# Last gates, split of y, conditioning columns and GpSimd work in a decoder trunk

## The chip, the cores and the metric

The kernel runs on one core of a Trainium2 chip. The metric is the time of one execution on the device, in microseconds (us). Six engines matter here: PE (TensorE, matmuls), DVE (VectorE), ACT (ScalarE), POOL (GpSimd) and the queues of DMAs that SP (SyncE) and POOL issue. Each engine works its own instructions strictly in the order in which they stand; it waits at an instruction until what this needs is there.

## The reference, cut to what matters

A trunk of two layers over x of 1024 positions by 1024 channels. Each sub-layer is a norm with scale and shift from a conditioning vector, a mixer or an MLP, and a gated residual add:

```python
for i in range(2):
    mod = einsum("bd,de->be", silu(c), w_mod[i]) + b_mod[i]
    sh_m, sc_m, gt_m, sh_f, sc_f, gt_f = split(mod, 6)
    h = rms_norm(x, norm_mix_g[i]) * (1 + sc_m) + sh_m
    y = recurrent_mixer(h, ...) if i == 0 else pool_mixer(h, ...)
    x = x + gt_m * y
    h = rms_norm(x, norm_ffn_g[i]) * (1 + sc_f) + sh_f
    x = x + gt_f * (relu(h @ w1[i]) ** 2 @ w2[i])
out = rms_norm(x, final_norm_g)

def recurrent_mixer(h, ...):
    gate = gelu(h @ w_y + b_y)
    xr = causal_conv4(h @ w_in + b_in)
    r, g = sigmoid(heads(xr, w_a)), sigmoid(heads(xr, w_x))   # 4 heads of 256
    log_a = 8 * r * log_sigmoid(lam)
    xr = scan(exp(log_a), sqrt(-expm1(2 * log_a)) * g * xr)   # along the sequence
    return (xr * gate) @ w_out + b_out
```

All of it is float32.

## The kernel before

Activations lie transposed, 128 channels on the partitions and positions along the free axis, in two halves of 512 positions (h = 0 and 1; tiles `xa` and `xb`). A float32 product is made of three: an operand is split into a high part, rounded to a type that PE multiplies fast, and a low part, the rest. One 128x512 block over 1024 channels, `proj`, is thus 24 matmuls (lines 188 to 190). A high part is an ACT copy, a low part a DVE or POOL subtraction, or, for weights in the variant "dma" (`neg_part`), an ACT negation onto which a DMA of POOL's queue adds the weights once more.

Weights come as units of 512 KB by SP's queue into three raw buffers (`rawp`), and split into eight half-unit tiles (`wpool`). The conditioning vectors `mod[i, j]` are made of columns: `drip` loads 512 KB of `w_mod` into one of the same three raw buffers (tile `mb`) and multiplies and sums them on DVE (line 207). `rate[0]` says how many columns `split_unit` drips with each unit.

The mixer of layer 0 ends with four heads. Per head and half, `gates` splits its input (tile `xchl`, from a pool of 19 slots that `yh` and `yl` share), makes 24 matmuls, four sigmoids, and on ACT, POOL and DVE exp, tanh, square root and scan; `gelu_block` makes 48 matmuls, two gelus and the products. `split_y(h)` splits the result into `yh` and `yl`. Then the projection `w_out` runs in two groups of four output blocks, each over both halves; each block is evacuated by ACT, added to x by DVE and squared into a sum (`SumSq`) whose plan gives each addition to V (DVE) or G (POOL). `ffn_norm` adds up the sum on PE (line 272), broadcasts the reciprocal root (line 286), and `norm_split` makes `hh` and `hl`, for three of eight blocks (`lean`) with POOL. The FFN's first product `f1` of both halves follows, then `f2`.

A scheduler puts the instructions of each engine in order from the order in the code, its own estimates of when things are ready, and the free buffers; the lines alone don't show it.

Of the kernel before, what the change touches and what calls it, by code (L numbers as in the profile page):

```python
# [10 lines left out]
F32 = mybir.dt.float32  # L11
F32R = mybir.dt.float32r
AF = mybir.ActivationFunctionType
# [29 lines left out]
def trunk_kernel(ctx, tc, xT, vecs, wmod, w_k, w_in, w_y, w_g, w_out, w_p, w1, w2, outT):  # L43
    nc = tc.nc
    V, S, G, PE = nc.vector, nc.scalar, nc.gpsimd, nc.tensor
# [44 lines left out]
    x = [Blocks("xa"), Blocks("xb")]  # L90
# [66 lines left out]
    rate = [0]  # L157
# [10 lines left out]
    def split_unit(src, name, eng=None, drips=None):  # L168
        raw = load(src, name)
        drip(rate[0] if drips is None else drips)  # L170
        if eng == "dma":
            return [neg_part(raw[:, c:c + H], src[:, c:c + H], f"{name}_{c}") for c in (0, H)]
        return [split_part(raw[:, c:c + H], f"{name}_{c}", eng) for c in (0, H)]
# [26 lines left out]
    mod = {}  # L200
# [28 lines left out]
    def drip(n):  # L229
        for _ in range(n):  # L230
            next(steps, None)
# [56 lines left out]
            trace[S], trace[V] = root, last  # L288
        return bc

    def norm_split(x, bc, a, b, hh, hl, lean=()):
        for k in range(NB):
            t = tmp("nt")
            V.scalar_tensor_tensor(t, x[:, k, :], a[:, k:k + 1], bc, op0=ALU.mult, op1=ALU.mult)  # L294
            if k in lean:
                S.activation(t, t, AF.Identity, bias=b[:, k:k + 1])
                S.copy(hh[:, k, :], t)
                G.tensor_sub(hl[:, k, :], t, hh[:, k, :].bitcast(F32))
                continue
            last = (S.activation(hh[:, k, :], t, AF.Identity, bias=b[:, k:k + 1]),  # L300
                    V.scalar_tensor_tensor(hl[:, k, :], t, b[:, k:k + 1], hh[:, k, :].bitcast(F32),  # L301
                                           op0=ALU.add, op1=ALU.subtract))
        return last


    hh, hl = [None, None], [None, None]
# [11 lines left out]
    a, b = const.tile([P, NB], F32, name="amix0"), mod_tile(0, 0)  # L318
# [70 lines left out]
    for k in range(NB):  # L389
# [17 lines left out]
        for low, r in ((0, hh), (0, hl), (1, hh)):  # L407
            for u in range(6):
                w, c = (w1_, u * P) if u < 4 else (w2_, odd * 256 + (u - 4) * P)
# [101 lines left out]
    def gates(hd, unit, h):  # L511

        xchl = slot("xchl", (2, 2, H), F32R)
        xch, xcl = xchl[:, 0, :, :], xchl[:, 1, :, :]
        src = xc[h][:, 2 * hd:2 * hd + 2, :]
        S.copy(xch, src)
        V.tensor_sub(xcl, src, xch.bitcast(F32))
        rs, gs = [], []
        for mi in range(2):
            b = 2 * hd + mi  # L520
            for g in range(2):
                ps = acc_mm()
                for k in range(2):
                    mm3(ps, unit, ((g * 2 + k) * 2 + mi) * P, xch[:, k, :], xcl[:, k, :], k == 0, k == 1)
                t = tmp("gate")
                S.activation(t, ps, AF.Sigmoid, bias=vcol("ba" if g == 0 else "bx", b))
                (rs if g == 0 else gs).append(t)
        aa = []
        for mi in range(2):
            b = 2 * hd + mi  # L530

            av = tmp("a")
            S.activation(av, rs[mi], AF.Exp, scale=coef[:, b:b + 1])
            S.activation(rs[mi], rs[mi], AF.Tanh, scale=ncoef[:, b:b + 1])
            aa.append(av)
        for mi in range(2):
            e = tmp("asq")
            G.tensor_mul(e, aa[mi], aa[mi])  # L538
            V.scalar_tensor_tensor(rs[mi], e, 1.0, rs[mi], op0=ALU.add, op1=ALU.mult)
        for mi in range(2):  # L540
            b = 2 * hd + mi
            S.activation(rs[mi], rs[mi], AF.Sqrt)
            hs = xc[h][:, b, :]
            G.tensor_mul(gs[mi], gs[mi], hs)
            V.tensor_mul(gs[mi], gs[mi], rs[mi])
            V.tensor_tensor_scan(hs, aa[mi], gs[mi], 0.0 if h == 0 else carry[:, b:b + 1],
                                 op0=ALU.mult, op1=ALU.add)
            if h == 0:
                V.tensor_copy(carry[:, b:b + 1], hs[:, H - 1:H])
# [9 lines left out]
    def split_y(h):  # L559
        yh[h], yl[h] = Blocks(f"yh{h}", F32R), Blocks(f"yl{h}", F32R)  # L560
        for k in range(NB):
            S.copy(yh[h][:, k, :], xc[h][:, k, :])
            V.tensor_sub(yl[h][:, k, :], xc[h][:, k, :], yh[h][:, k, :].bitcast(F32))

    for hd in range(4):
        rate[0] = min(hd, 2)
        ug = split_unit(w_g[hd], f"g{hd}")
        uy = [split_unit(w_y[m], f"y{m}") for m in (2 * hd, 2 * hd + 1)]
        for h in range(2):
            gates(hd, ug, h)  # L570
            for mi in range(2):
                gelu_block(2 * hd + mi, uy[mi], h)
            if hd == 3:
                if h == 1:
                    wo = [split_unit(w_out[m], f"o{m}", G, 0) for m in range(4)]
                split_y(h)

    af = [None, None]

    def ffn_norm(i, h, ss):  # L580
        if af[i] is None:
            drip_until(i, 3)
            af[i] = norm_scale(vcol(f"gffn{i}"), mod[i, 4], f"affn{i}")
        bc = rstd_bcast(ss)
        new_h(h)
        norm_split(x[h], bc, af[i], mod[i, 3], hh[h], hl[h], (1, 3, 5))


    drip_until(0, 2)
    gtb = const.tile([P, NB], F32, name="gtb")  # L590
    V.tensor_mul(gtb, mod[0, 2], vcol("bout"))
    room = slot("ssq")
    ss = [SumSq("f00", plan="GVGVGVGV", room=room[:, 0:2, :]), SumSq("f01", plan="GVGVGVGV", room=room[:, 2:4, :])]
    rate[0] = 4
    for m0 in (0, 4):
        if m0:
            wo = [split_unit(w_out[m], f"o{m}") for m in range(m0, m0 + 4)]
        for h in range(2):
            for m in range(m0, m0 + 4):
                ps = proj(wo[m - m0], yh[h], yl[h])  # L600
                t = tmp("wo")
                S.activation(t, ps, AF.Identity, bias=gtb[:, m:m + 1], scale=mod[0, 2][:, m:m + 1])
                V.tensor_add(x[h][:, m, :], x[h][:, m, :], t)
                ss[h].add(x[h][:, m, :])
                if h == 1 and m == 4:
                    ffn_norm(0, 0, ss[0])

# [81 lines left out]
    def f1_jobs(i, c, eng=None):  # L689
        return [partial(lambda j: split_unit(w1[i, c * 4 + j], f"w1_{i}_{c}_{j}", eng, DRIPS[j]), j) for j in range(4)]  # L690
# [166 lines left out]
    def jobs(i, first, last):  # L857

        for c in range(first, last):
            yield from f1_jobs(i, c, G if (i, c) == (0, 0) else None)  # L860
            yield from f2_jobs(i, c)
        yield from f1_jobs(i, last)

# [93 lines left out]

    sa, sb = SumSq("n0a", plan="GVGVGVGV"), SumSq("n0b", plan="VVVVVVVV")  # L960
    qa, qb = SumSq("f1a", plan="VVVVVVVV"), SumSq("f1b", plan="VVVVVVVV")
    f1(0, 6, AB, fast=True, ahead=ahead)
    drip_until(1, 5)
# [67 lines left out]
    sa = last_chunk(0, 0, H, "GVGVGVGV")  # L1031
    sb = last_chunk(1, 0, n1, "VVVVVVVV", once(lambda: final_norm(rstd_bcast(sa), 0, 0, H)))
# [73 lines left out]
```

## Time and profile before

| | us |
|---|---|
| median of 3 runs | 1766.14 (1762.34 to 1766.17) |
| profiled execution | 1766.89 |
| its span on the core | 1765.1 |
| PE busy | 1704.2 (97%) |
| DVE busy | 1367.9 (77%) |
| ACT busy | 959.7 (54%) |
| POOL busy | 544.3 (31%) |

A busy share is a mean over stages with different limits. PE's idle 61 us lie in a few places, and a matmul counts as busy at either clock, so the granted clock is to be read beside it. The heads of the mixer take about 130 to 275 us of the span, the projection 275 to 371, `f1` of the first FFN chunk 371 to 426.

### The profile page before, as it was taken

The numbers are of one execution on the slowest core, as the hardware profiler recorded it, in microseconds if no ns is written. First come the engines' busy times: TensorE is split into PE (matmuls) and PEld (weight loads), VectorE is DVE, ScalarE is ACT, GpSimd is POOL, SyncE is SP. The second block draws the span as 40 slices with busy tenths as digits, with TensorE's granted clock in tenths as the row PEclk, the third lists the DMA queues.
The fourth block names the chain that finished last, engine by engine and source line by source line (L and its number), as shares of the span: only waits on it lengthen the run. The fifth ranks groups of instructions, "written<-read, shape, count | busy, mean of one in ns | idle before, by whom it ended". The sixth has DMA issues, their size and how long they took to land.

```text
span 1765.1 us, 20959 instructions
## 1 busy us (share of the span) xinstructions
PE 1704.2 (97%) x7510; PEld 1397.7 (79%) x7510; DVE 1367.9 (77%) x2092; ACT 959.7 (54%) x1648; POOL 544.3 (31%) x442
## 2 busy tenths in 40 slices
PE   5899989989999999999999999999999999999997
PEld 3687768778788888888888888888878787878787
DVE  8898866678888888888874698649786968686836
ACT  4578884346354545444456688745444454545432
POOL 4323332151313223241407433312231404140403
PEclk8999999989999999999999999999999999999998
DMA  9223413521424142423217889861111111111202
GB/s 354 90 72 107 144 60 108 190 84 48 140 71 135 60 143 72 132 73 118 84 48 166 196 182 194 171 167 47 61 37 60 54 42 60 48 61 36 78 7 96
DMA packets 59577, 180.80 MB, mean 102 GB/s; under 512 B 6352, under 2 KB 8784, under 8 KB 59472
## 3 DMA queue, kind: packets, MB, share of 16 engines
q1 hardware_dynamic: 47376, 157.43, 27.7%
q0 software_dynamic: 12096, 22.03, 7.5%
q8 instruction: 59, 0.97, 0.2%
q14 instruction: 46, 0.38, 0.1%
HBM read 175.24 MB, written 4.19 MB: 102 GB/s over the span
## 4 chain that ended last, share of the span: by engine, by line
PE 71%; DVE 15%; ACT 5%; DMA 4%; issue 3%; POOL 1%; SPq 0%; DVEq 0%; ACTq 0%; POOLq 0%
PE mm L188 23%; PE mm L189 23%; PE mm L190 23%; DMA mb<-in_wmod 3%; DVE mb L207 2%; DVE mw L333 1%; DVE xca L449 1%; DVE xa L780 1%; PE sm L272 1%; DVE xb L780 1%; POOL xa L789 1%; DVE xcb L449 1%; DVE hl L301 1%; DVE nt L294 1%; POOL asq L538 1%
## 5 line engine op out<-in xcount | busy, mean ns | idle before, releaser
L188 PE MATMUL mm<-hh,w_w 128*128 128x512 f32 x1024 | 400.3, 391 | 1.0 <-DVE xa L780 1.0
L189 PE MATMUL mm<-hl,w_w 128*128 128x512 f32 x1024 | 399.4, 390 | 0.0
L190 PE MATMUL mm<-hh,w_w 128*128 128x512 f32 x1024 | 399.3, 390 | 0.0
L789 POOL TENSOR_TENSOR xb<-xb,c 128x512 f32<-128x512 f32 x104 | 149.8, 1440 | 603.9 <-ACT c L784 558.9
L188 PEld LDWEIGHTS mm<-hh,w_w 128*128 128x128 f32 x1024 | 192.8, 188 | 42.5 <-DVE xa L780 2.7
L190 PEld LDWEIGHTS mm<-hh,w_w 128*128 128x128 f32 x1024 | 192.8, 188 | 40.4
L189 PEld LDWEIGHTS mm<-hl,w_w 128*128 128x128 f32 x1024 | 192.8, 188 | 39.8
L789 POOL TENSOR_TENSOR xa<-xa,c 128x512 f32<-128x512 f32 x104 | 160.0, 1538 | 145.0 <-ACT c L784 145.0
L784 ACT ACTIVATE c<-c,mod 128x512 f32<-128x512 f32 x104 | 75.3, 724 | 204.5 <-DVE c L810 119.0
L207 DVE SCALAR_TENSOR_TENSOR mb<-mb,cond 128x1024 f32<-128x1024 f32 x80 | 115.3, 1442 | 53.7 <-DMA mb<-in_wmod 53.5
L630 ACT ACTIVATE relu<-mm 128x512 f32<-128x512 f32 x128 | 76.3, 596 | 140.8 <-PE mm L190 140.7
L780 DVE SCALAR_TENSOR_TENSOR xa<-mm,mod,xa 128x512 f32<-128x512 f32 x156 | 113.0, 742 | 25.8 <-POOL xa L789 21.0
L181 DVE TENSOR_TENSOR w_w<-raw_w,w_w 128x512 fp32r<-128x512 f32 x112 | 108.5, 977 | 12.0 <-ACT w_w L180 11.7
L165 POOL DMA_DIRECT2D w_w<-in_w x72 | 63.9, 906 | 106.6 <-ACT w_w L164 65.9
L180 ACT CAST w_w<-raw_w 128x512 fp32r<-128x512 f32 x120 | 69.8, 612 | 27.9 <-PE mm L190 20.6
L620 DVE TENSOR_TENSOR u<-usq,u 128x512 fp32r<-128x512 f32 x102 | 70.3, 689 | 17.1 <-ACT u L619 16.7
L188 PE MATMUL mm<-u,w_a_a 128*128 128x512 f32 x200 | 79.1, 396 | 2.2 <-DVE xa L780 1.0
L188 PE MATMUL mm<-u,w_w 128*128 128x512 f32 (+1 forms) x224 | 81.0, 362 | 0.0
L189 PE MATMUL mm<-u,w_w 128*128 128x512 f32 (+1 forms) x224 | 80.6, 360 | 0.1
L190 PE MATMUL mm<-u,w_w 128*128 128x512 f32 (+1 forms) x224 | 80.4, 359 | 0.0
L189 PE MATMUL mm<-u,w_a_a 128*128 128x512 f32 x200 | 78.0, 390 | 0.0
L190 PE MATMUL mm<-u,w_a_a 128*128 128x512 f32 x200 | 77.9, 389 | 0.0
(336 smaller groups left out, 4113.9 us busy)
## 6 DMA issues: line engine op xcount, KB each, us to landing
raw_w<-in_w SPq DMA_DIRECT2D x148, 512.0 KB, 3.6
mb<-in_wmod SPq DMA_DIRECT2D x80, 512.0 KB, 3.7
w_w<-in_w POOLq DMA_DIRECT2D x72, 256.0 KB, 5.5
mw<-in_wmod SPq DMA_DIRECT2D x16, 512.0 KB, 9.2
raw_in<-in_w_in SPq DMA_DIRECT2D x8, 512.0 KB, 3.6
raw_y<-in_w_y SPq DMA_DIRECT2D x8, 512.0 KB, 3.6
raw_o<-in_w_out SPq DMA_DIRECT2D x8, 512.0 KB, 3.7
outT<-o SPq DMA_DIRECT2D x12, 256.0 KB, 2.3
```

Of the source, the lines that this page charges most:

```text
L165: nc.gpsimd.dma_start(w[:, 1, 0:n], src, accum_op=ALU.add)
L180: S.copy(w[:, 0, 0:n], raw)
L181: (eng or V).tensor_sub(w[:, 1, 0:n], raw, w[:, 0, 0:n].bitcast(F32))
L188: PE.matmul(out=ps, lhsT=wh, rhs=rh, start=first, stop=False)
L189: PE.matmul(out=ps, lhsT=wh, rhs=rl, start=False, stop=False)
L190: PE.matmul(out=ps, lhsT=w[:, 1, c:c + P], rhs=rh, start=False, stop=last)
L207: V.scalar_tensor_tensor(raw, raw, 1.0, cond, op0=ALU.mult, op1=ALU.mult, accum_out=m[:, e:e + 1])
L620: eng.tensor_sub(u[n][:, 1, jj, :], src, u[n][:, 0, jj, :].bitcast(F32))
L630: S.activation(r, ps, AF.Relu)
L780: V.scalar_tensor_tensor(xb, ps, g[:, r + 4 * row:r + 4 * row + 1], xb, op0=ALU.mult, op1=ALU.add)
L784: S.activation(t, src, AF.Identity, scale=g[:, r + 4 * row:r + 4 * row + 1])
L789: G.tensor_add(xb, xb, t)
```

## The change

`norm_split` loses `lean`: all eight blocks go the same way, ACT for `hh` and DVE for `hl`. The plans of three sums give all additions to DVE. The weights of the projection's second group and of the FFN's first chunk are split by "dma" instead of by DVE and by POOL. The columns' rate is 0, 1, 2, 3 in the heads (before 0, 1, 2, 2), one after each block of the projection's first group, and 0 with its second group's units (before 4 each). `split_y(0)` stands after the last gates, and the first four units of `w_out` and `split_y(1)` after the heads.

```diff
-    def norm_split(x, bc, a, b, hh, hl, lean=()):
+    def norm_split(x, bc, a, b, hh, hl):
         for k in range(NB):
             t = tmp("nt")
             V.scalar_tensor_tensor(t, x[:, k, :], a[:, k:k + 1], bc, op0=ALU.mult, op1=ALU.mult)
-            if k in lean:
-                S.activation(t, t, AF.Identity, bias=b[:, k:k + 1])
-                S.copy(hh[:, k, :], t)
-                G.tensor_sub(hl[:, k, :], t, hh[:, k, :].bitcast(F32))
-                continue
...
     for hd in range(4):
-        rate[0] = min(hd, 2)
+        rate[0] = hd
         ug = split_unit(w_g[hd], f"g{hd}")
         uy = [split_unit(w_y[m], f"y{m}") for m in (2 * hd, 2 * hd + 1)]
         for h in range(2):
             gates(hd, ug, h)
+            if (hd, h) == (3, 1):
+                split_y(0)
             for mi in range(2):
                 gelu_block(2 * hd + mi, uy[mi], h)
-            if hd == 3:
-                if h == 1:
-                    wo = [split_unit(w_out[m], f"o{m}", G, 0) for m in range(4)]
-                split_y(h)
+    wo = [split_unit(w_out[m], f"o{m}", G, 0) for m in range(4)]
+    split_y(1)
...
-        norm_split(x[h], bc, af[i], mod[i, 3], hh[h], hl[h], (1, 3, 5))
+        norm_split(x[h], bc, af[i], mod[i, 3], hh[h], hl[h])
...
-    ss = [SumSq("f00", plan="GVGVGVGV", room=room[:, 0:2, :]), SumSq("f01", plan="GVGVGVGV", room=room[:, 2:4, :])]
-    rate[0] = 4
+    ss = [SumSq("f00", plan="VVVVVVVV", room=room[:, 0:1, :]), SumSq("f01", plan="VVVVVVVV", room=room[:, 1:2, :])]
+    rate[0] = 0
     for m0 in (0, 4):
         if m0:
-            wo = [split_unit(w_out[m], f"o{m}") for m in range(m0, m0 + 4)]
+            wo = [split_unit(w_out[m], f"o{m}", "dma") for m in range(m0, m0 + 4)]
         for h in range(2):
             for m in range(m0, m0 + 4):
...
                 ss[h].add(x[h][:, m, :])
+                if m0 == 0:
+                    drip(1)
                 if h == 1 and m == 4:
                     ffn_norm(0, 0, ss[0])
...
-            yield from f1_jobs(i, c, G if (i, c) == (0, 0) else None)
+            yield from f1_jobs(i, c, "dma" if (i, c) == (0, 0) else None)
...
-    sa, sb = SumSq("n0a", plan="GVGVGVGV"), SumSq("n0b", plan="VVVVVVVV")
+    sa, sb = SumSq("n0a", plan="VVVVVVVV"), SumSq("n0b", plan="VVVVVVVV")
```

How the scheduler moves the instructions is shown at three places. The line numbers of the changed kernel are five lower from `norm_split` to the projection and three lower behind it.

**The heads, DVE.** Around the scan of head 3, first half, before; `xchl<-xcb` is the input of its second half, `yl` a low part of y:

```order
L539 SCALAR_TENSOR_TENSOR gate<-asq,gate 128x512 x2
L545 TENSOR_TENSOR gate<-gate 128x512 x2
L546 SCALAR_TENSOR_TENSOR xca_469<-a,gate 128x512 x2
L549 COPY carry<-xca_469 128x1 x2
L555 TENSOR_TENSOR xca_469<-xca_469,gelu 128x512
L517 TENSOR_TENSOR xchl<-xcb_471,xchl 128x1024
```

The same instruction now, before the scan of head 2, first half, with the columns (`mb`, line 207) that follow up to the gates of head 2, second half:

```order
L512 TENSOR_TENSOR xchl<-xcb_471,xchl 128x1024
L540 TENSOR_TENSOR gate<-gate 128x512 x2
L541 SCALAR_TENSOR_TENSOR xca_469<-a,gate 128x512 x2
L544 COPY carry<-xca_469 128x1
L207 SCALAR_TENSOR_TENSOR mb_4_6_1826,mod_4_1559<-mb_4_6_1826,cond 128x1024
L544 COPY carry<-xca_469 128x1
L550 TENSOR_TENSOR xca_469<-xca_469,gelu 128x512 x2
L207 SCALAR_TENSOR_TENSOR mb_4_7_1837,mod_4_1559<-mb_4_7_1837,cond 128x1024
L181 TENSOR_TENSOR w_y_0_1829<-raw_y_1818,w_y_0_1829 128x512
L210 TENSOR_TENSOR mod_4_1559<-mod_4_1559,vec 128x8
L240 SCALAR_TENSOR_TENSOR affn_2626<-mod_4_1559,vec 128x8
L207 SCALAR_TENSOR_TENSOR mb_3_0_1842,mod_3_1841<-mb_3_0_1842,cond 128x1024
```

The split of the last gates' input moved some 30 instructions forward, and columns `mb_4_7` and `mb_3_0`, which before stood behind `split_y(1)`, now stand ahead of the gates of head 2, second half, on DVE.

**The projection's second group, first half, DVE.** Before, from its first block on (`xa`, the residual add; `ssq`, the sum of squares):

```order
L207 SCALAR_TENSOR_TENSOR mb_5_5_2462,mod_5_2438<-mb_5_5_2462,cond 128x1024
L603 TENSOR_TENSOR xa_82<-xa_82,wo 128x512
L207 SCALAR_TENSOR_TENSOR mb_5_6_2465,mod_5_2438<-mb_5_6_2465,cond 128x1024
L207 SCALAR_TENSOR_TENSOR mb_5_7_2794,mod_5_2438<-mb_5_7_2794,cond 128x1024
L603 TENSOR_TENSOR xa_82<-xa_82,wo 128x512
L210 TENSOR_TENSOR mod_5_2438<-mod_5_2438,vec 128x8
L263 TENSOR_TENSOR ssq<-ssq,sq 128x512
L207 SCALAR_TENSOR_TENSOR mb_1_0_2807,mod_1_2806<-mb_1_0_2807,cond 128x1024
L603 TENSOR_TENSOR xa_82<-xa_82,wo 128x512 x2
L263 TENSOR_TENSOR ssq<-ssq,sq 128x512
```

Now:

```order
L207 SCALAR_TENSOR_TENSOR mb_5_3_2797,mod_5_2393<-mb_5_3_2797,cond 128x1024
L598 TENSOR_TENSOR xa_82<-xa_82,wo 128x512
L263 TENSOR_TENSOR ssq<-ssq,sq 128x512
L598 TENSOR_TENSOR xa_82<-xa_82,wo 128x512
L263 TENSOR_TENSOR ssq<-ssq,sq 128x512
```

The last pair stands twice more behind these. The columns between the adds are gone there, and every addition of squares stands on DVE.

**The second norm's sum, DVE.** Before, the last adds of the second half (`xb`), up to the reciprocal; `raw_w` are FFN weights:

```order
L603 TENSOR_TENSOR xb_84<-xb_84,wo 128x512
L263 TENSOR_TENSOR ssq<-ssq,sq 128x512
L603 TENSOR_TENSOR xb_84<-xb_84,wo 128x512
L207 SCALAR_TENSOR_TENSOR mb_1_2_2829,mod_1_2806<-mb_1_2_2829,cond 128x1024
L729 TENSOR_TENSOR raw_w_0_0_0_2838<-raw_w_0_0_0_2838 128x256
L603 TENSOR_TENSOR xb_84<-xb_84,wo 128x512
L731 TENSOR_TENSOR raw_w_0_0_0_2838<-raw_w_0_0_0_2838 128x256
L263 TENSOR_TENSOR ssq<-ssq,sq 128x512
L207 SCALAR_TENSOR_TENSOR mb_1_3_2840,mod_1_2806<-mb_1_3_2840,cond 128x1024
L729 TENSOR_TENSOR raw_w_0_0_1_3194<-raw_w_0_0_1_3194 128x256
L276 RECIPROCAL rstd<-rstd 128x4
```

Now:

```order
L207 SCALAR_TENSOR_TENSOR mb_5_5_2823,mod_5_2393<-mb_5_5_2823,cond 128x1024
L263 TENSOR_TENSOR ssq<-ssq,sq 128x512
L598 TENSOR_TENSOR xb_84<-xb_84,wo 128x512
L726 TENSOR_TENSOR raw_w_0_0_0_2834<-raw_w_0_0_0_2834 128x256
L728 TENSOR_TENSOR raw_w_0_0_0_2834<-raw_w_0_0_0_2834 128x256
L263 TENSOR_TENSOR ssq<-ssq,sq 128x512
L207 SCALAR_TENSOR_TENSOR mb_5_6_2836,mod_5_2393<-mb_5_6_2836,cond 128x1024
L598 TENSOR_TENSOR xb_84<-xb_84,wo 128x512
L207 SCALAR_TENSOR_TENSOR mb_5_7_3183,mod_5_2393<-mb_5_7_3183,cond 128x1024
L263 TENSOR_TENSOR ssq<-ssq,sq 128x512
L210 TENSOR_TENSOR mod_5_2393<-mod_5_2393,vec 128x8
```

Before, one column stood here ahead of the last addition; now three do, and there is one addition more.

## Rows read from the trace of the kernel before

**Rows 1.** Waits of PE, 120 to 400 us: total us, times, longest us.

```profile
engine line waited for: us in total, times, longest us
PE mm L188 <- ACT xchl L516: 5.7, 1, 5.7
PE sm L272 <- POOL ssq L263: 4.9, 2, 2.7
PE mm L188 <- ACT gelu L554: 4.0, 4, 1.5
PE sm L272 <- DVE ssq L263: 3.4, 2, 1.9
```

**Rows 2.** Stretches: length, PE busy (matmuls), PE's granted clock, DMA share, GB/s.

```profile
255.30:260.60 5.30, 4.89 (x11) 0.50 0.00 0
...
349.80:356.50 6.70, 6.70 (x23) 0.50 0.00 0
...
382.00:390.60 8.60, 8.58 (x27) 0.50 0.21 69
...
1130.00:1320.00 190.00, 189.96 (x837) 1.00 0.33 85
```

**Rows 3.** Timeline of PE: start us, us, line, out<-in, count; where stages begin.

```profile
249.22 0.39 PE L190 MATMUL mm<-hh,w_y 128*128 128x512 f32 x1
...
274.77 0.39 PE L188 MATMUL mm<-yh,w_o 128*128 128x512 f32 x1
...
371.49 0.39 PE L188 MATMUL mm<-hh,w_w 128*128 128x512 f32 x1
...
426.28 0.39 PE L188 MATMUL mm<-u,w_a_a 128*128 128x512 f32 x1
```

**Rows 4.** Timeline of DVE and ACT in heads 2 and 3, with idle time before.

```profile
226.68 1.22 DVE L207 SCALAR_TENSOR_TENSOR mb<-mb,cond 128x1024 f32<-128x1024 f32 x1 [2.29 <-DMA mb<-in_wmod]
...
235.00 0.69 DVE L539 SCALAR_TENSOR_TENSOR gate<-asq,gate 128x512 f32<-128x512 f32 x1 [0.93 <-POOL asq L538]
...
254.25 1.03 ACT L516 CAST xchl<-xcb 128x1024 fp32r<-128x1024 f32 x1
...
259.94 1.28 ACT L526 ACT_TABLE_LOAD   x1 [0.47 <-PE mm L190]
```

**Rows 5.** Timeline of DVE and POOL at the end of the projection's first half.

```profile
338.60 1.23 DVE L207 SCALAR_TENSOR_TENSOR mb<-mb,cond 128x1024 f32<-128x1024 f32 x1 [1.62 <-DMA mb<-in_wmod]
...
339.75 0.69 DVE L603 TENSOR_TENSOR xa<-xa,wo 128x512 f32<-128x512 f32 x1
...
343.89 1.23 DVE L207 SCALAR_TENSOR_TENSOR mb<-mb,cond 128x1024 f32<-128x1024 f32 x1 [2.06 <-DMA mb<-in_wmod]
...
347.09 1.25 DVE L603 TENSOR_TENSOR xa<-xa,wo 128x512 f32<-128x512 f32 x1 [1.36 <-ACT wo L602]
...
346.53 1.26 POOL L263 TENSOR_TENSOR ssq<-ssq,sq 128x512 f32<-128x512 f32 x1 [8.40 <-ACT sq L262]
```

**Rows 6.** Timeline of DVE between the first norm and the second's sum.

```profile
369.12 3.47 DVE L301 SCALAR_TENSOR_TENSOR hl<-nt,mod,hh 128x512 fp32r<-128x512 f32 x2
...
376.26 2.31 DVE L207 SCALAR_TENSOR_TENSOR mb<-mb,cond 128x1024 f32<-128x1024 f32 x1
```

**Rows 7.** Prices: DMA issues and operations by line, ns min/median/max, landing us.

```profile
mb<-in_wmod SPq DMA_DIRECT2D x80, 512.0 KB, 3.7
...
L165 POOL DMA_DIRECT2D w_w<-in_w x72: 852/872/1667, 938.7 to 1165.9; - x72
...
DMA to landing us min/median/max: 3.8/5.6/8.3
...
1124.03 0.95 PE L272 MATMUL sm<-ones,ssqf1bV 128*128 128x1 f32 x8
...
L301 DVE SCALAR_TENSOR_TENSOR hl<-nt,mod,hh x28: 736/747/1989, 85.4 to 1138.9; 128x512 fp32r<-128x512 f32 x28
```

**Rows 8.** Stretches: length, busy of PE, PEld, DVE, ACT, POOL; clock, DMA, GB/s.

```profile
190.00:250.00 60.00, 58.09 (x254) 47.12 (x252) 45.13 (x62) 54.00 (x76) 25.20 (x18) 1.00 0.38 123
402.00:426.00 24.00, 24.00 (x107) 19.88 (x106) 18.82 (x33) 14.94 (x27) 0.00 (x0) 1.00 0.15 44
```

## The prediction

> **What bounds the kernel now.** PE is busy in 1704 of 1765 us, so only the places where it stands still or runs slowly are worth anything. I read first who PE waited for between 120 and 400 us [rows 1]: once 5.7 us for ACT's copy `xchl` of the last gates, 4.0 us in four pieces for gelu evacuations, and 8.3 us (4.9 and 3.4) at the two sums of squares `ssq` of the next norm. Then the granted clock after each long wait [rows 2]: 0.50, the lower of the two levels (1.2 of 2.4 GHz), from 255.3 to 260.6, from 349.8 to 356.5 and from 382.0 to 390.6. Each long wait is thus paid twice. From 1130 to 1320 PE does 837 matmuls in 189.96 us, 0.227 us each, with no wait: the pace that I charge for undisturbed work. Then when PE starts each stage [rows 3]: its last gelu matmul of head 3, first half, at 249.22, the projection `w_o` at 274.77, the FFN's first product at 371.49, its second at 426.28.
>
> **The ideal.** (A) From 249.45 to the projection stand 24 gate and 48 gelu matmuls, 72 x 0.227 = 16.3 us, so 265.8 instead of 274.77: 9.0 us lost. (B) The projection is 16 blocks of 24, 384 x 0.227 = 87.1 us; with one part of the sum of squares the small matmuls L272 are 8 for 0.95 us [rows 7], the broadcast adds about 0.5: 88.5 against 96.7, 8.2 us lost. (C) The first FFN product is 8 blocks, 43.5 us, plus 1.4 for the second norm's small matmuls: 44.9 against 54.8, 9.9 us lost. More than 27.1 us is not there in these places.
>
> **The change, part by part.**
>
> *Last gates.* ACT casts `xchl` of (3, 1) only at 254.25, after its chain of (3, 0) [rows 4]; the pool of slots is the reason that I read from the code, since the first half's `yh`, `yl` take four slots before it. In the new order `split_y(0)` comes after these gates, and the cast and its subtraction move ahead of the scan of (2, 0), some 35 us earlier. The wait for `xchl` goes. Next late is the ACT chain: between 190 and 250 it is busy 54.0 of 60 us [rows 8], and PE can run ahead of it by six PSUM buffers. Following that chain, the first gelu of (3, 0) frees its buffer about 0.5 us after PE asks for it: 0.5 off.
>
> *Columns in the heads.* Rate 3 instead of 2 puts three more columns into DVE's queue there, 3 x 1.23 us, and their 512 KB loads into SP's ahead of `raw_y` 7. DVE already stands 2.29 us for a column at 226.68 [rows 4]. `mb_4_7` and `mb_3_0` now come through one free buffer, one after the other: `mb_4_6` is done about 224.4, 3.7 us to land [rows 7] and 1.2 to work gives 229.4 and then about 234.4, in front of the first gate operation L539, whose second of the pair moves from 235.00 to about 236.4. The subtractions of `yl` that stood there (3.3 us) have left, or it would be worse. So 1.4 us go to ACT's square root behind it and to PE; from 0, if a buffer comes free sooner, to 5, one more round trip. With the 0.5 above, 2 us off: A gives 7.0.
>
> *Projection.* Before, 16 columns stand between the residual adds of all blocks, 5.3 us apart at 338.60 and 343.89 [rows 5], so the add of the last block of the first half comes at 347.09, though PE finished it near 340, and at 1.25 us instead of 0.69, beside POOL's addition that starts at 346.53. Now the second half has no column behind `mb_5_3`. The first half has seven, and behind `split_y(1)` three raw buffers turn them over; I get the last at about 298, some 15 us after PE ended the block whose add waits behind it, and six PSUM buffers hold 33 us of blocks. When PE asks for the sum at T + 70.7 (T the projection's start), the last sum is ready at about T + 68. B gives its 8.2. Eight DVE subtractions become 8 ACT negations (beside 5.4 us blocks in which ACT has 1.4 us of other work) and 8 transfers from POOL's queue. The first low half: its unit is loaded only behind `mb_5_1`, negated at about 302.5, plus 0.87 us of issue and 5.6 to land [rows 7] = 309; PE wants it at 311.4. Covered by 2 us.
>
> *Norm.* POOL's subtractions and additions go. DVE gets 3 more operations of 0.75 us per norm and 4 more additions per sum, each the size of the add of 0.69 [rows 5]; against that, two L301 took 3.47 us beside POOL's work where their median is 0.747 [rows 6, 7]. The Trainium skill, page "SBUF — State Buffer", section "SBUF: two separate sides", says that the port pair DVE shares with GpSimd is an exclusive lock; that agrees with the 3.47. The same section's box warns that a DVE operation can also keep GpSimd from writing descriptors for its own DMAs, which speaks against the 16 transfers put there; it is a rival below.
>
> *Second norm's sum.* PE reaches it half a block later in the new order. Its chain on DVE has `mb_5_5`, `mb_5_6`, `mb_5_7` in front of the last adds, as `mb_1_2` stood before at 376.26 for 2.31 us [rows 6]. I follow it to T + 97.5 where PE asks at T + 96.9: 1 us off, 0 to 5. C gives 8.9.
>
> *Behind it.* The second norm's output ends some 4 to 5 us later against PE's second half than before, where DVE is busy 18.8 of 24 us [rows 8]. The idle 5.2 us hide it or don't: 0 to 5 off, I take 2.5, the middle.
>
> *Elsewhere.* The pool mixer's first sum loses 8 of 16 small matmuls: 0.95 us won. Three DVE operations more in each norm of the second layer cost nothing while PE doesn't wait there; from 1130 on it has none [rows 2]. The columns end three units later, before their first use. If that cover failed, 3 x 0.75 us each.
>
> **Sum.** The profiled execution took 1766.89 us, 1.8 more than its span; the median of the runs is 1766.14, 0.04% lower, so I don't correct. 7.0 + 8.2 + 8.9 - 2.5 + 0.9 = 22.5: 1766.9 - 22.5 = **1744.4 us**. With the costs at zero it is 27.1 + 0.9 = 28 us, 1738.9. With all at their ends (5.5, 5 and 5, so 3.5 + 8.2 + 4.9 - 5 + 0.9 = 12.5) it is 1754.4.
>
> **Rivals.**
>
> *ACT holds the heads* (chance 0.11). The earlier copy brings nothing, because ACT's chain, 54.0 of 60 us busy, and not `xchl`, sets when PE may go on. For: PE already waits 4.0 us for gelu [rows 1]. Against: ACT's table load at 259.94 waited for PE [rows 4], so ACT could have gone on sooner. A falls out: 1766.9 - 15.5 = 1751.4.
>
> *The second norm's chain stays late* (0.11). The columns 5_5 to 5_7 wait for buffers held by FFN weights, one round trip of 5 us each past the first; PE waits over 4 us at the sum, the clock falls as it did after 382.0, and C is gone: 1766.9 - 13.6 = 1753.3.
>
> *Low halves late* (0.06). If DVE keeps POOL from issuing, an issue takes 1.67 us and 8.3 to land, the longest [rows 7]: 302.5 + 10.0 = 312.5, 1.1 us behind PE, for up to 8 units (their cycle of load, cast and transfer is not shorter than PE's block): about 9 us, 1753.4. By the figures of the Trainium skill, page "SBUF — State Buffer", section "A bandwidth-pool intuition that's wrong (but worth ruling out)", 0.62 us alone and 3.1 beside a DVE copy, an estimate has the first low half 2.5 us later, at 311.5, and the sum would stay. What decides is that 72 such issues have a median of 0.872 in stages where DVE is at work too.
>
> *Two of these together* (0.08): 1760 to 1763, no change that can be told.
>
> *Slower* (0.04). The projection's columns find a single raw buffer, because two hold `raw_o` units that wait for weight tiles. Then the seven columns behind 286 come at 5.3 us each, as at 338.60 and 343.89 [rows 5], the last at 323; unit 4 is loaded behind it and its low half lands 3.7 + 1.2 + 0.9 + 5.6 = 11.4 us later, at 334.4, where PE wants it at 311.4: 23 us, 4 more at the lower clock. With C gone too, the second norm's columns being served alike: 1744.4 + 27 + 8.9 = 1780. It decides if `raw_o` 2 and 3 are still uncast when `mb_3_3` is due; I have them cast at about 277, ten microseconds before.
>
> **How the numbers follow.** The forecast, with its costs between their ends (1738.9 to 1754.4), has 0.60. A measurement of this kernel tells about 0.3%, 5.3 us, from no change: faster is below 1760.8. Faster: 0.60 + 0.11 + 0.11 + 0.06 = 0.88; same 0.08; slower 0.04. The range leaves out the last two: 1739 to 1757, the forecast with the single rivals and their costs.
>
> **What would show it.** A: no wait of PE for `xchl`, and the projection's first matmul near 267.8; later than 272 means the first rival. B: no wait of L272 at the first sum and a clock of 1.00 there; the FFN starts 88.5 us after the projection. C: the second product 46 us after that, with at most 1 us of wait at the second sum. Waits of `w_o` matmuls for DMA would show the third rival, DVE idle for `mb` between the first adds the fourth. The whole is wrong if PE meets a new wait over 4 us, since the clock then doubles the price.

## The result and the profile after

The changed kernel takes **1748.06 us** (median of 4 executions, 1747.45 to 1752.28) beside 1764.88 of the kernel before: a ratio of 0.9914, interval 0.9896 to 0.9933, 0.9% faster. The forecast was 1744.4 with a range of 1739 to 1757. The profiled execution took 1752.28 us, its span is 1750.5 us, 14.6 less than before. It is the slowest of the four executions.

The waits of PE between 120 and 400 us, total, times and longest, which answer to [rows 1]:

```profile
engine line waited for: us in total, times, longest us
PE mm L188 <- ACT gelu L549: 5.6, 4, 1.8
PE sm L272 <- DVE mod L210: 4.0, 1, 4.0
```

The waits for `xchl` and for GpSimd's sum are gone. Gelu waits have grown from 4.0 to 5.6 us, and one sum, the second, still waits. The stage starts on PE, as in [rows 3] (start, duration, line, out<-in):

```profile
240.96 0.50 PE L188 MATMUL mm<-hh,w_y 128*128 128x512 f32 x1 [1.84 <-ACT gelu L549]
...
269.92 0.39 PE L188 MATMUL mm<-yh,w_o 128*128 128x512 f32 x1
...
340.64 0.95 PE L272 MATMUL sm<-ones,ssq 128*128 128x1 f32 x8
...
358.38 0.39 PE L188 MATMUL mm<-hh,w_w 128*128 128x512 f32 x1
...
370.96 1.66 PE L272 MATMUL sm<-ones,ssq 128*128 128x1 f32 x8 [4.03 <-DVE mod L210]
...
410.77 0.39 PE L188 MATMUL mm<-u,w_a_a 128*128 128x512 f32 x1
```

The first sum starts without a wait, with 8 small matmuls instead of 16; the second waits 4.03 us. PE's granted clock behind the two waits that are left (length, busy, clock, DMA share, GB/s), against [rows 2]:

```profile
242.00:245.00 3.00, 3.00 (x9) 0.52 0.12 15
346.00:357.00 11.00, 11.00 (x50) 1.00 0.91 195
372.00:377.50 5.50, 5.50 (x15) 0.50 0.26 84
```

The lower level, 1.2 GHz, now stands behind a gelu wait and behind the second sum; behind the first sum the clock is 1.00.

All kernels of this study side by side, from their traces. *Heads* runs from the first gate matmul of head 0 to the projection's first matmul, *projection* from there to the FFN's first product, *first product* to the second product, *rest* to the end of the span. The last column is the median of each kernel's times.

| kernel | heads | projection | first product | sum | rest | time |
|---|---|---|---|---|---|---|
| before | 144.76 | 96.72 | 54.79 | 296.27 | 1338.82 | 1764.88 |
| changed | 138.98 | 88.46 | 52.39 | 279.83 | 1339.73 | 1748.06 |
| e11 changed again | 138.75 | 88.46 | 52.55 | 279.76 | 1339.38 | 1748.48 |
| e1 order alone | 135.41 | 105.40 | 54.91 | 295.72 | 1338.50 | 1763.96 |
| e2 heads' columns out | 135.93 | 89.63 | 52.07 | 277.63 | 1338.32 | 1747.46 |
| e3 second sum free | 139.07 | 99.14 | 45.05 | 283.26 | 1337.78 | 1750.93 |
| e4 GpSimd back | 138.08 | 89.48 | 53.75 | 281.31 | 1338.87 | 1751.05 |
| e5 columns in second group | 138.01 | 92.94 | 45.01 | 275.96 | 1338.38 | 1747.66 |
| e6 and heads | 135.01 | 98.51 | 45.97 | 279.49 | 1338.36 | 1748.17 |
| e7 columns back | 135.26 | 104.56 | 50.96 | 290.78 | 1338.35 | 1762.28 |
| e8 DVE and GpSimd split | 139.29 | 90.21 | 51.53 | 281.03 | 1339.05 | 1751.76 |
| e9 columns early | 138.61 | 92.29 | 44.99 | 275.89 | 1338.08 | 1745.74 |
| e10 columns earlier | 139.88 | 88.47 | 44.99 | 273.34 | 1339.52 | **1742.03** |
| e12 third in head 2 | 140.52 | 96.77 | 45.01 | 282.30 | 1337.99 | 1751.34 |

The kernels ran on several chips; beside the experiments the kernel before took 1765.13 to 1765.97 us. What stands ahead of head 0 differs by up to 3 us between the traces (the first gate matmul starts at 127.9 to 130.9), by 1.1 between the two of the changed kernel itself. So for differences of 1 to 3 us the stages tell more than the times. But each kernel has one trace, only the changed kernel two, and both of these show its slowest execution, 4.2 and 2.3 us above the median: a stage that is a microsecond or two better than the changed kernel's is no gain in time yet.

### The profile page after: what moved, and what is told of

It reads as the page before. It is cut to its first block, busy times and chain, and to the rows that moved or that the text cites. A ratio compares the mean times of both kernels' runs of the same rounds, so it can differ in the third digit from the quotient of the medians.

```text
span 1750.5 us, 20898 instructions
## 1 busy us (share of the span) xinstructions
PE 1695.7 (97%) x7486; PEld 1391.5 (79%) x7486; DVE 1369.4 (78%) x2108; ACT 962.4 (55%) x1652; POOL 519.2 (30%) x429
## 4 chain that ended last, share of the span: by engine, by line
PE 73%; DVE 15%; ACT 4%; issue 3%; DMA 3%; POOL 1%; DVEq 0%; SPq 0%; ACTq 0%; POOLq 0%
PE mm L188 24%; PE mm L189 24%; PE mm L190 24%; DMA mb<-in_wmod 2%; DVE mb L207 2%; DVE mw L328 1%; DVE xa L777 1%; DVE xb L777 1%; POOL xa L786 1%; DVE xca L444 1%; DVE xcb L444 1%; DVE w_a_s L181 1%; ACT c L781 1%; DMA raw_k<-in_w_k 1%; PE sm L272 0%
## 5 line engine op out<-in xcount | busy, mean ns | idle before, releaser
L190 PE MATMUL mm<-hh,w_w 128*128 128x512 f32 x1024 | 399.3, 390 | 0.0
L190 PEld LDWEIGHTS mm<-hh,w_w 128*128 128x128 f32 x1024 | 192.8, 188 | 40.4
L207 DVE SCALAR_TENSOR_TENSOR mb<-mb,cond 128x1024 f32<-128x1024 f32 x80 | 116.2, 1455 | 47.2 <-DMA mb<-in_wmod 47.0
L777 DVE SCALAR_TENSOR_TENSOR xa<-mm,mod,xa 128x512 f32<-128x512 f32 x156 | 113.0, 742 | 25.2 <-POOL xa L786 25.2
L165 POOL DMA_DIRECT2D w_w<-in_w x80 | 70.5, 899 | 151.3 <-ACT w_w L164 119.4
L617 DVE TENSOR_TENSOR u<-usq,u 128x512 fp32r<-128x512 f32 x102 | 70.2, 688 | 16.1 <-ACT u L616 15.8
L190 PE MATMUL mm<-u,w_w 128*128 128x512 f32 (+1 forms) x224 | 80.4, 359 | 0.0
L180 ACT CAST w_w<-raw_w 128x512 fp32r<-128x512 f32 x112 | 65.1, 612 | 24.0 <-PE mm L190 17.3
L190 PE MATMUL mm<-u,w_a_a 128*128 128x512 f32 x200 | 77.9, 389 | 0.0
```

Source lines behind the costliest of these rows:

```text
L165: nc.gpsimd.dma_start(w[:, 1, 0:n], src, accum_op=ALU.add)
L180: S.copy(w[:, 0, 0:n], raw)
L190: PE.matmul(out=ps, lhsT=w[:, 1, c:c + P], rhs=rh, start=False, stop=last)
L207: V.scalar_tensor_tensor(raw, raw, 1.0, cond, op0=ALU.mult, op1=ALU.mult, accum_out=m[:, e:e + 1])
L617: eng.tensor_sub(u[n][:, 1, jj, :], src, u[n][:, 0, jj, :].bitcast(F32))
L777: V.scalar_tensor_tensor(xb, ps, g[:, r + 4 * row:r + 4 * row + 1], xb, op0=ALU.mult, op1=ALU.add)
```

## Experiments

**The order of the gates, alone (e1), and the columns in the heads (e2).** e1 is the kernel before with only the new order:

```diff
             gates(hd, ug, h)
+            if (hd, h) == (3, 1):
+                split_y(0)
...
-            if hd == 3:
-                if h == 1:
-                    wo = [split_unit(w_out[m], f"o{m}", G, 0) for m in range(4)]
-                split_y(h)
+    wo = [split_unit(w_out[m], f"o{m}", G, 0) for m in range(4)]
+    split_y(1)
```

> The kernel before with the new order of the last gates and of split_y alone; columns, weight splits and sums as before. Theory (the wait for xchl is the whole loss, and the three columns in the heads cost the changed kernel some 3 us): no wait for xchl, gelu waits of 0.7 to 0.8 us as before, the projection starts at about 266.5 instead of 274.77, both sums of the next norm wait as before, the time is some 8 us below the kernel before, near 1757. Rival (ACT's chain, not the columns, holds the heads in the changed kernel): gelu waits of 1.4 to 1.8 us here too, projection at 269.5 or later, near 1760. Second rival (the lead is given back): the columns among the adds of the projection come no sooner, the first sum waits longer, and the time is within 2 us of the kernel before.

Time 1763.96 us beside 1765.45, ratio 0.999 (0.998 to 0.9999): next to nothing. The heads are 9.35 us shorter, the projection is 8.68 longer, so the second rival was right. PE's waits in e1 from 264 to 380 us, and DVE on the way to the first sum:

```profile
PE sm L272 <- POOL ssq L263: 11.3, 2, 8.6
PE sm L272 <- DVE ssq L263: 3.2, 2, 1.9
PE mm L188 <- ACT w_o L180: 1.5, 1, 1.5
```

```profile
336.83 0.69 DVE L603 TENSOR_TENSOR xa<-xa,wo 128x512 f32<-128x512 f32 x1
...
341.30 1.23 DVE L207 SCALAR_TENSOR_TENSOR mb<-mb,cond 128x1024 f32<-128x1024 f32 x1 [2.39 <-DMA mb<-in_wmod]
342.45 0.08 DVE L207 DVE_READ_ACCUMULATOR mb<-mb,cond 128x1 f32 x1
342.45 0.69 DVE L603 TENSOR_TENSOR xa<-xa,wo 128x512 f32<-128x512 f32 x1
344.50 1.26 DVE L603 TENSOR_TENSOR xa<-xa,wo 128x512 f32<-128x512 f32 x1 [1.36 <-ACT wo L602]
```

The adds stand behind columns that wait for their transfers (14.1 us in ten waits between 300 and 346), and the last add comes at 344.50 instead of 347.09 [rows 5]. PE starts the projection 11.1 us sooner (1.7 of it from ahead of the heads), but the sum comes only 2.6 us sooner. The new order alone is worth next to nothing.

e2 is the changed kernel with the three columns moved out of head 3:

```diff
-        rate[0] = hd
+        rate[0] = min(hd, 2)
...
-                    drip(1)
+                    drip(2 if h == 1 and m < 3 else 1)
```

> The changed kernel with two columns per unit in the last head as before, and the three columns instead behind blocks 0 to 2 of the projection's first group, second half. Theory (the columns make the gelu waits of the heads, 1.45 and 1.84 us, and the low clock behind the second): the waits fall to 0.7 to 0.8, the clock between 240 and 245 is back at 1.00, the projection starts at 266.6 instead of 269.92, and 3.3 us less in all, near 1744.8. Rival (split_y(0) on ACT and DVE makes them): the waits stay, the projection stays within 0.7 of 269.9, near 1748.

The heads shrink by 3.05 us, and of PE's waits from 200 to 300 us one is left:

```profile
PE mm L188 <- ACT gelu L549: 1.5, 1, 1.5
```

The wait of 1.84 in head 3 is gone, with the low clock; the one in head 2 (1.45 in the changed kernel) stays. So the third column per unit made the one and not the other, half theory, half rival. e1, without the third column, has the wait in head 2 too (1.32, against 0.73 before): it came with the new order. The projection gives 1.2 us back: PE waits 0.87 us for a low half of `w_o`, the cover that the prediction put at 2 us. The time, 1747.46 us, can't be told from the changed kernel's.

**What the first sum was late for (e7, e4, e8).** e7 puts the columns back where they were, e4 GpSimd's additions and subtractions, e8 the two splits of weights:

```diff
-        rate[0] = hd
+        rate[0] = min(hd, 2)
...
-    rate[0] = 0
+    rate[0] = 4
...
-                if m0 == 0:
-                    drip(1)
```

> The changed kernel with the columns where they were before: two per unit in the last head, four per unit of the projection's second group, none in its first. Split by DMA and no GpSimd work stay. Theory (columns among the adds made the first sum late): the projection starts at 266, the first sum waits 5 us or more for DVE's addition, the clock falls behind it, the FFN starts 94 us or more after the projection, 1752 to 1758. Rival (DVE's subtractions of the weights and GpSimd's work made it late, not the columns): wait under 2 us, 1745 to 1748.

> The changed kernel with GpSimd's share given back: sums of the two halves and of the pool mixer's norm added by both engines in turn, and three of eight blocks of a norm subtracted on GpSimd. Theory (the first sum was late for the columns between the adds, not for GpSimd): three times 8 more small matmuls, 2.9 us, and at most 2 us of wait, 1751 to 1753. Rival (GpSimd was the cause): the first sum waits 4 us or more for a GpSimd addition, the clock falls, 1756 or more.

> The changed kernel with weights split as before: DVE subtracts for the projection's second group, GpSimd for the FFN's first chunk. Theory (the transfers only relieve DVE where it has room): first sum within 1 us of 70.7 behind the projection's start, second sum as late as in the changed kernel or up to 2 us later, 1747 to 1750. Rival (the eight subtractions or GpSimd's work hold the adds): a new wait of 2 us or more at the first sum, 1753 or more.

e7: 1762.28 us, ratio to before 0.9984 (0.9974 to 0.9993); the projection takes 104.56 us, 16.1 more than in the changed kernel. The size is beyond the theory's (1752 to 1758), and the place is another. PE's waits, 264 to 390 us:

```profile
PE mm L190 <- DMA w_o<-in_w_out: 8.7, 2, 7.7
PE sm L272 <- DVE ssq L263: 5.4, 2, 4.2
PE mm L188 <- ACT w_o L163: 2.4, 1, 2.4
```

PE waits for low halves of weights. Their units are loaded among 16 columns through the same three raw buffers, and with the split by DMA the low half is a second transfer behind that. Of the waits for DVE's sums 1.2 us stand at the first and 4.2 at the second. So e7 shows what the columns' place is worth, but not that it acts through the adds: that is read from the traces of the kernel before [rows 5] and of e1, where the weights are not split by DMA.

e4 costs 1751.05 us, 3.0 more by the times; the stages show 1.0 in the projection (8 small matmuls more, no wait at the first sum) and 1.4 in the first product, where the second sum waits 2.9 us, for GpSimd's addition. The theory holds for the first sum: GpSimd was named in [rows 1] for 4.9 us, but its additions were only the last to end, behind late adds.

e8 costs 1751.76 us. The first sum comes 70.72 us behind the projection's start, to the hundredth as in the changed kernel, then a broadcast waits 1.4 us for DVE's `dg`, and the second sum is as late as there (3.87 us). So there is no new wait of 2 us, as in the theory, but the time lies above the theory's range (1747 to 1750) and below the rival's. By the stages the split by DMA is worth 1.75 us in the projection and 0.9 over projection and first product; what makes up the rest of the 3.7 us of time is not shown.

**The second sum (e3, e5, e6).** The six columns that come with the FFN's first weights lose their place, and seven are put in earlier: in e3 behind the blocks of the projection's first group, in e5 behind those of its second group, first half; e6 is e5 with two columns per unit in head 3 and so ten there. In all three, `f1_jobs` and the first two `f2_weights` of chunk 0 get no column, and

```diff
                 if m0 == 0:
-                    drip(1)
+                    drip(2 if h == 0 or m < 3 else 1)
```

in e3, and in e5

```diff
                 if m0 == 0:
                     drip(1)
+                elif h == 0:
+                    drip(2 if m < 7 else 1)
```

> The changed kernel without columns in front of the second norm's sum: none with the four units of the FFN's first product and the first two of its second, seven more behind the projection's first blocks. Theory (columns waiting for their transfers hold the last adds): the second sum doesn't wait, the clock stays at 1.00, the FFN's second product starts 46 us after its first instead of 52.4, 6.4 us less in all, near 1741.7. Rival (DVE's three more operations per norm and the additions hold the sum): a wait of 3 us or more stays, near 1748. Second rival: the seven columns delay the first norm's sum, a wait of 2 us or more appears at it, and half of the gain or more is lost.

> The changed kernel with the seven columns in front of the second norm's sum put elsewhere again: behind the blocks of the projection's second group, first half, so that their loads stand behind those of w_out and ahead of those of the FFN's weights. Theory (in e3 the columns took the raw buffers from the units of w_out; here they take them from FFN weights that have no tile to go to yet): no wait of w_o matmuls, the first sum 70.7 us after the projection's start with under 1 us of wait, no wait at the second sum, the second product 45 to 46 us after the first, 6.4 us less than the changed kernel, near 1741.7. Rival (any column among the adds of the second group holds the first sum): a wait of 2 us or more at it, the clock falls behind it, near 1746. Second rival: the FFN's weights come too late, the first product waits for them, 1745 or more.

> e5 with two columns per unit in the last head, so ten columns instead of seven behind the second group's blocks. Theory (both costs are columns and add up): projection at 3.3 to 3.7 us less than in the changed kernel, the rest as in e5, near 1738. Rival (ten are too many there): a wait of 2 us or more at the first sum or of the first product for weights, no better than e5.

In e3 and e5 the first product takes 45.0 us: no wait at the second sum, 7.4 us less than in the changed kernel and 9.8 less than before. That is the whole of what the prediction put as C's ideal (9.9), so the columns are the cause: DVE's extra operations of the norm and the additions are still there. But the projection pays. In e3 it takes 10.7 us more; SP's queue of the changed kernel first, e3's second (start, time to the last of the group, count):

```profile
272.46 22.23 SPq L222 DMA_DIRECT2D mb<-in_wmod  x8
296.11 9.75 SPq L99 DMA_DIRECT2D raw_o<-in_w_out  x4
```

```profile
269.53 35.41 SPq L222 DMA_DIRECT2D mb<-in_wmod  x15
306.85 7.00 SPq L99 DMA_DIRECT2D raw_o<-in_w_out  x4
```

With fifteen columns ahead of them the units of `w_out` are loaded 10.7 us later (13.7 later counted from the projection's start, which came 3.0 sooner), and PE waits:

```profile
318.99 0.80 PE L190 MATMUL mm<-yh,w_o 128*128 128x512 f32 x1 [6.26 <-DMA w_o<-in_w_out]
```

In e5, where they stand behind these units, the `w_o` waits are absent and the first sum waits 2.68 us for DVE's addition, with the lower clock behind it: 4.5 of the 7.4 us are lost again. In e6, with ten, the first sum waits 6.3 us and the three microseconds won in the heads are gone too. By the times e3 (1750.93) is 2.5 to 2.9 us slower than the changed kernel; e5 (1747.66) and e6 (1748.17) can't be told from it, though by the stages e5 is 3.9 us ahead.

**The changed kernel again (e11).**

> The changed kernel itself, unaltered, beside the two others on the same chip. Its first profile had a clock of 0.66 behind the gelu wait of head 3 and two waits of 0.70 and 0.67 us in the fifth chunk's second product, and that execution was the slowest of four by 4 us. If these are chance, a second profile lacks one of them or both, its span is 1.5 to 4 us shorter, and the second sum's wait of 4 us stays; if they belong to the order, all three are there again.

1748.48 us, ratio 0.9898 (0.988 to 0.9917). PE's waits from 120 to 1700 us:

```profile
PE mm L188 <- DVE xa L777: 6.9, 7, 1.0
PE mm L188 <- ACT gelu L549: 5.4, 4, 2.0
PE sm L272 <- DVE mod L210: 4.2, 1, 4.2
PE mm L188 <- DVE xb L777: 1.3, 4, 0.6
```

The second sum's wait and the low clock behind the gelu wait of head 3 are there again. Of the two waits of 0.70 and 0.67 us in the second product of the sixth FFN chunk (the expectation counts it from zero, as the fifth) one of 0.55 is. That stage takes 40.2 and 39.0 us in the two traces, 38.1 before.

The clock in head 3 fell behind waits of 1.84, 1.89, 1.92 and 1.96 us (changed, e8, e3, e11) and not behind 1.92 and 2.23 (e5, e4). Three microseconds behind that wait in e11, then in e5 (length, busy, clock, DMA share, GB/s):

```profile
241.00:244.00 3.00, 3.00 (x9) 0.51 0.21 29
...
242.00:245.00 3.00, 3.00 (x15) 1.00 0.14 19
```

So the length of the wait alone doesn't decide it, and what does stays open. It is worth 1.6 us from that gelu matmul to the next gates (12.6 against 11.0).

**A better order of the same columns (e9, e10, e12).** The two costs found, three columns in head 3 and those before the second sum, ask for other places. Per unit in heads 0 to 3, in the projection's first and second group, and with the four units of the FFN's first product (the changed kernel has two more with the first units of its second product, the others none):

```text
changed  0 1 2 3   8   0   1 1 1 1
e9       0 2 2 2   9   6   none
e10      1 2 2 2  10   0   1 1 0 0
e12      0 1 3 2  10   3   1 1 0 0
```

> The changed kernel with the columns spread once more: 0, 2, 2, 2 per unit in the four heads (changed kernel 0, 1, 2, 3), nine in the projection's first group, six behind the first three blocks of its second, none before the second norm's sum. Theory (the gelu wait of head 3 goes with its third column per unit, the second sum's wait with the columns before it; six columns with the second group cost less than the seven of e5): projection 61.6 us after the gelu product of head 2, first half, FFN 90 to 92 us behind it, second product 45 us behind that, 7 to 10 us less from stage to stage than the changed kernel, near 1740. Rival (columns have no room anywhere before the FFN): head 1 waits longer for gelu or the first sum waits 2.7 us or more as in e5, near 1747.

> The same aim with 1, 2, 2, 2 per unit in the heads, ten columns in the projection's first group, two with the first two units of the FFN as in the changed kernel, none before the second norm's sum. Theory: first sum as in the changed kernel (under 1 us of wait, FFN 88.5 to 90 us behind the projection), second product 45 us behind the first, projection 61.6 us after the gelu product of head 2, near 1738, if the three columns more in head 0 cost nothing. Rival (DVE is full around heads 0 and 1, from 90 to 120 us it is busy 29.9 of 30): PE waits there, the stage of head 2 starts 2 us or more later than the other kernels' 201.6 to 204.5, near 1742 or more.

> The aim of e9 and e10 with 0, 1, 3, 2 columns per unit in the four heads, ten in the projection's first group, three with its second, two with the first two units of the FFN, none before the second norm's sum. Theory (a column costs where DVE has no room: heads 0 and 1 in e9 and e10, head 3 in the changed kernel; head 2 and the projection have room): the stage of head 2 starts at 201.6 to 204.5 as in the changed kernel, the first sum waits under 1 us, the second product starts 45 us after the first, at about 400, near 1740. Rival (a third column per unit costs as much in head 2 as in head 3): gelu waits of 1.8 us and a low clock there, 3 to 4 us later, near 1743. Second rival: thirteen columns in the projection are too many, a first sum's wait of 2 us or more, near 1743 too.

e10 takes **1742.03 us** (1741.41 to 1744.95), ratio 0.9868 (0.9852 to 0.9884): each of its four executions is below each of e11's four on the same chip (1747.00 to 1750.75). Projection as in the changed kernel, first product 44.99. Between 100 and 420 us PE waits in one place only:

```profile
PE mm L189 <- DVE xchl L512: 6.9, 1, 6.9
```

DVE there, the columns among the convolution's last operations and the input of head 0's first gates:

```profile
127.38 1.23 DVE L207 SCALAR_TENSOR_TENSOR mb<-mb,cond 128x1024 f32<-128x1024 f32 x1 [0.71 <-DMA mb<-in_wmod]
...
133.10 1.22 DVE L207 SCALAR_TENSOR_TENSOR mb<-mb,cond 128x1024 f32<-128x1024 f32 x1 [0.31 <-DMA mb<-in_wmod]
...
136.34 1.22 DVE L512 TENSOR_TENSOR xchl<-xca,xchl 128x1024 fp32r<-128x1024 f32 x1
```

The rival named this place and the time, 1742. The lower clock follows (0.50 from 137.6 to 141.0). But behind it no gelu wait is left in any head, so most of the price comes back: the heads take 139.88, 0.9 more than in the changed kernel. e9 gains the second sum and loses 3.8 us in the projection, where the first sum waits 2.03. e12 shows both its rivals: gelu waits of 3.1 and 0.5 us in head 2 and 4.8 us at the first sum, where three of the columns ahead wait 3.7 to 4.0 us each for their transfers. So two columns more cost nothing in the projection's first group (88.47 in e10); three, six and seven in its second group (e12, e9, e5) each came with a wait at the first sum; and the wait in head 0 was the one that was given back.

## Why the prediction was right, point by point

The sign was right and the time lies in the range: 16.4 us by the stages (296.27 - 279.83) and 16.8 by the medians, against 22.5 forecast. In the profiled span it is 14.6, since the heads start 0.9 later and *rest* takes 0.9 longer. That the time came out within 4 us of the forecast is in part luck: one of three main terms, C, fell short by 6.5 us, a loss of 2.5 that was taken off did not come, and the range had been laid wide enough to hold a failure of C alone. The steps:

- **A, last gates: 5.8 instead of 7.0.** The ideal of 9.0 was right: with two columns per unit in head 3 the heads shrink by 8.8 to 9.75 us (e2, e1, e6). The columns' path was right too. DVE and ACT there in the changed kernel:

```profile
233.75 1.23 DVE L207 SCALAR_TENSOR_TENSOR mb<-mb,cond 128x1024 f32<-128x1024 f32 x1 [1.79 <-DMA mb<-in_wmod]
...
237.56 0.68 DVE L534 SCALAR_TENSOR_TENSOR gate<-asq,gate 128x512 f32<-128x512 f32 x1
...
238.27 0.63 ACT L537 ACTIVATE gate<-gate 128x512 f32<-128x512 f32 x1 [2.02 <-DVE gate L534]
238.93 1.28 ACT L549 ACT_TABLE_LOAD   x1
240.22 0.69 ACT L549 ACTIVATE gelu<-mm,vec 128x512 f32<-128x512 f32 x1
```

  Without the 0.9 us by which this execution's heads started later, the last of the columns ends at 234.1 (235.0 here, forecast 234.4) and the second gate operation of the pair starts at 236.6 (237.56, forecast 236.4); gelu follows through ACT. What was mis-sized is the price: three columns cost 3.05 us (138.98 - 135.93), priced at 1.4 and the ACT chain at 0.5, since the low clock behind the wait (0.52) was not counted, though the prediction says itself that long waits are paid twice. Where the clock didn't fall (e4, e5), they cost 2.1.
- **B, first sum: 8.26 instead of 8.2.** The FFN starts 88.46 us behind the projection (forecast 88.5), no wait, clock 1.00. That the columns' place makes the gain, and neither GpSimd's share nor the split of the weights, is shown by e7 against e4 and e8: put back one at a time, they cost 16.1, 1.0 and 1.75 us of projection. That the columns act through the adds is read from traces. What the prediction did not say: A is no gain by itself. e1 has A without B and is worth 1.5 us in time; B without A was not run.
- **C, second sum: 2.4 instead of 8.9.** This step failed, and the second rival took its place, with its wait over 4 us and its clock (0.50); only its price was too high, since 2.4 us of C came all the same. The chain was put at T + 97.5; PE asked at T + 97.0 and got it at T + 101.0. DVE before that sum:

```profile
366.56 1.23 DVE L207 SCALAR_TENSOR_TENSOR mb<-mb,cond 128x1024 f32<-128x1024 f32 x1 [3.09 <-DMA mb<-in_wmod]
367.71 0.08 DVE L207 DVE_READ_ACCUMULATOR mb<-mb,cond 128x1 f32 x1
367.71 0.69 DVE L598 TENSOR_TENSOR xb<-xb,wo 128x512 f32<-128x512 f32 x1
368.97 1.23 DVE L207 SCALAR_TENSOR_TENSOR mb<-mb,cond 128x1024 f32<-128x1024 f32 x1 [0.58 <-DMA mb<-in_wmod]
370.12 0.08 DVE L207 DVE_READ_ACCUMULATOR mb<-mb,cond 128x1 f32 x1
370.12 0.69 DVE L263 TENSOR_TENSOR ssq<-ssq,sq 128x512 f32<-128x512 f32 x1
370.73 0.16 DVE L210 TENSOR_TENSOR mod<-mod,vec 128x8 f32<-128x8 f32 x1
```

  and what SP's queue waited for from 340 to 375 us:

```profile
SPq L222 <- ACT w_w L163: 21.3, 3, 15.6
SPq L222 <- DVE mb L207: 7.8, 2, 6.7
```

  The columns' loads (L222) stood 21.3 us for raw buffers that ACT's casts of FFN weights (L163) had to free, and four of the eight casts had in turn waited for PE's matmuls (L190). The loads of the last two columns were issued at 359.23 and 360.74, and the slower took 8.2 us to land, where the prediction elsewhere takes 3.7 for a load. How much of the delay is buffers and how much landing is not shown. The forecast of T + 97.5 states no term for either, the wait for buffers stands only in the second rival: to leave both out was the error. By the prediction's own sign, at most 1 us of wait at this sum, C was wrong. e3, e5, e9 and e10 show that the full 9.8 us were there.
- **Behind it: 0 instead of 2.5 lost.** The second product takes 40.9 us in both kernels (467.19 - 426.28 and 451.68 - 410.77), with two waits of 0.9 to 1.0 us that were there before, and in the first product PE waits for nothing but the second sum.
- **Elsewhere.** The stage with the pool mixer's sum is 0.8 us shorter (0.9 forecast). The cover of the late columns was costed at nothing and failed in one place: in the second product of the sixth chunk a column (L207, at 858.80, 2.31 us beside GpSimd's work) stands on DVE right in front of the evacuation `xb` (L777, at 861.04) that PE waits for; before, no column is left there. That stage lost 2.0 and 0.9 us in the changed kernel's two traces. *rest* is 1339.4 to 1339.7 there and 1337.8 to 1339.1 in all others but e10, so part of this is chance, and how much stays open.
- **Low halves.** In time in the changed kernel (no wait of a `w_o` matmul), late as soon as PE came 3.7 us sooner (e2, 0.87 us) or more columns stood before their units (e3, e7). The mechanism was not the issue on GpSimd that the third rival named, but the load of the unit. That rival leaned on the Trainium skill, page "SBUF — State Buffer", section "SBUF: two separate sides", by which a DVE operation in a mode that uses two ports keeps GpSimd from writing descriptors. The trace shows no such stall behind the DVE operations here (mostly `scalar_tensor_tensor` and `tensor_tensor` on float32): DVE is busy 12.57 of 14 us from 344 to 358, and the issues from 346 on took 0.87 us in the median, as before:

```profile
L165 POOL DMA_DIRECT2D w_w<-in_w x7: 865/874/1133, 346.1 to 360.3; - x7
```

## What to carry to other kernels

Ask of a filler operation, such as a column here, not only what it takes but when its data comes. On an engine that runs in order, a 1.2 us operation in front of the last add can cost the wait for its transfer as well, and that wait depends on who holds the buffers that its load needs, here weights that themselves waited for PE. Two waits in a row on one chain have to be looked at together: taking the first away moved 9 us to the second (e1), and the gain came only with both gone. When a filler has to stand somewhere, look for a place where the bottleneck engine gets the wait back later (e10), rather than one where the filler's own engine merely looks idle.

## What the runs showed of the hardware

A wait of 1.84 to 1.96 us on PE, in one place of nearly the same kernel, was followed by the lower clock in four traces (0.50 for some 3 us) and by full clock in two, with waits of 1.92 and 2.23. In the changed kernel a column's load of 512 KB took 5.2 us to land in the median of the five between 340 and 375 us, where DMA was busy 0.91 of the time from 346 to 357, against 3.7 us over the whole kernel before [rows 7].
